# A diffusion backbone in fp32 on one core: taps laid out by the host, gate sums as columns, factors and modulation rows turned by transposes

## The chip, the cores and the metric

One core of a Trainium2 chip. The metric is the device time of one execution in microseconds, the median over the runs. The engines are named as in the profile: PE is TensorE's matrix multiply, PEld its weight load, DVE VectorE, ACT ScalarE, POOL GpSimd, SP SyncE, which issues nearly all the transfers of this kernel.

## What is computed

Two layers over 1024 latent rows of 1024 channels, with a context of 256 rows. The first is attention in a window of 128 with a sink and rotary positions, the second a conformer module with a depthwise convolution of 31 taps. Both begin with an RMS norm that is modulated by a shift and a scale, and end with a gate, all three made from the conditioning vector c.

```python
def reference(x, c, ctx, c_ctx, ada_w, ada_b, norm_g, attn_w_in, attn_sink, attn_w_out,
              conv_w_in, conv_b_in, conv_dw_w, conv_dw_b, conv_ln_g, conv_ln_b, conv_w_out, final_g):
    silu_c, silu_cc = jax.nn.silu(c), jax.nn.silu(c_ctx)
    for i in range(DEPTH):                      # 0: attention, 1: convolution
        shift, scale, gate = jnp.split((silu_c @ ada_w[i] + ada_b[i])[:, None, :], 3, axis=-1)
        h_lat = modulate(rmsnorm(x, norm_g[i]), shift, scale)        # h * (1 + scale) + shift
        if kind == 0:                           # h_ctx: the same of the context, with silu_cc
            y, y_ctx = attention_layer(h_lat, h_ctx, attn_w_in[j], attn_sink[j], attn_w_out[j], cos, sin, ctx_out)
        else:
            y = conformer_conv_branch(h_lat, *conv_args)
        x = x + gate * y
    return rmsnorm(x, final_g)

def conformer_conv_branch(h, w_in, b_in, dw_w, dw_b, ln_g, ln_b, w_out):
    a, gl, z = jnp.split(h @ w_in + b_in, 3, axis=-1)
    u = a * jax.nn.sigmoid(gl)
    u = depthwise_conv(u, dw_w) + dw_b          # 31 taps a channel, 2048 channels
    u = jax.nn.silu(layernorm(u, ln_g, ln_b))
    return (u * jax.nn.silu(z)) @ w_out
```

## The kernel before, in words

Every large product is made in three: each operand is split in a high and a low part of a rounded fp32 type, and high by high, low by high and high by low add up in PSUM (hh_page, hl_page with whi_page, wlo_page in attention's projections; h2h_page, h2l_page in the convolution's; gs_page, ozh_page, ozl_page with woh_page, wol_page in the output projections). These 512-column products make up most of what TensorE does. The small products that the change is about are plain fp32, and each of them stands in the trace as two records; a transpose stands as one.

- **Prologue.** The rows of x are normed and turned, k step by k step (kt 0 to 7). In the meantime `ada_mm` (line 408) makes shift and scale of the first layer as rows: for a k step of 256 channels four partial sums stand in partitions 0, 32, 64 and 96, c and the context's c in two neighbouring rows each. VectorE copies that to arow_half (`ada_row`, 420). `ada_cols` (424) makes columns of it: two plain products with `sel`, a 128x2 table of ones, add up the four partial sums and turn them at once; two operations on VectorE add the bias and write `mod`. Behind these stands the chain of x's tile: hf_page and hh_page (x times scale plus shift), hl_page (their difference), and TensorE's products. The upper half of x is scaled by a row of factors `rb1` instead: line 619 spreads the four columns of r1 over 128 partitions by four plain products with the identity.
- **Attention.** 16 heads by 8 blocks, with the projections' products filled in between (`fill`). The rest of the conditioning, `ada_rest` (672), runs beside it on VectorE: for 16 groups of 256 columns (four gate groups of layer 0, then the twelve groups of layer 1, of which the last four are its gate) eight multiply-adds over loads of ada_w, a copy to acc_a, and then a sum over the 128 partitions on TensorE. For shift and scale of layer 1 this is two products of 128x1, whose columns are copied to `mod1` (707 to 709). For a gate it is one product of ones with the row of 256, a copy of that row and a transfer to `gd` in HBM (702 to 705). `gate_rows` (1374) reads `gd` later, spread over the partitions (gate_page), for the output projections.
- **Taps.** At the end of attention the two tables dwr_page are cleared on POOL, the taps are loaded into their first 31 rows, and `turn_taps` (1390) turns them in four steps, each of four transposes and a copy to `dww`, between the products of attention's output projection (`later`). `sum_taps` (1424) then makes `wsum`, the sums of neighbouring taps. dww and wsum lie in the memory that `ada_rest` used for its loads (660).
- **Convolution and norm.** TensorE makes the projections of 16 channel blocks, VectorE, POOL and ACT the taps (`conv_dve`, `conv_pool`), and then `layer_norm` (1553) for two halves of the rows; it spreads its factor r by four plain products with the identity (1588), multiplies sixteen pages by it, and the output projection follows.

The order of the engines is the program's own: line 91 is the helper that pins an instruction of an engine in program order, so nearly all instructions carry this line in the profile, and they are told apart by their tiles. A scheduler places what isn't pinned, loads on SP among them.

Of the kernel before, what the change touches and what calls it, by code (L numbers as in the profile page):

```python
# [9 lines left out]
F32 = mybir.dt.float32  # L10
F32R = mybir.dt.float32r
AF = mybir.ActivationFunctionType
ALU = mybir.AluOpType

P = 128
# [10 lines left out]
NJ = CW // P  # L26
TAPS = 31
# [69 lines left out]
def backbone_kernel(  # L97
    ctx_stack: ExitStack,
    tc: tile.TileContext,
    x, ctx, ada_w, attn_sink, attn_w_out, conv_dw_w, conv_w_out, final_g,  # L100
    k_rows, k_vecs, k_ada, k_win, k_wconv, k_xt,
    k_cos, k_sin, k_mask, k_ident,
    out,
):
# [28 lines left out]
    def ps_o(i=None):  # L133
        if i is None:
            oflip[0] ^= 1
            i = oflip[0]
        return ps.tile([P, 512], F32, tag=f"o{i}", name=nm("pso"), bufs=1)
# [10 lines left out]
    def ctile(shape, dt, name):  # L148
        return cpool.tile(shape, dt, tag=name, name=name, bufs=1)
# [7 lines left out]
    def tt(eng, out, a, b, op):  # L157
        return eng.tensor_tensor(out=out, in0=a, in1=b, op=op)
# [10 lines left out]
    sink = ctile([P, 16], F32, "sink")[:, 0:NH]  # L169
    nsink = ctile([P, NH], F32, "nsink")  # L170
    ones = ctile([P, P], F32, "ones")
    dww = ctile([P, NJ, TAPS], F32, "dww")
    pt = ptpool.tile([P, 5280], F32R, tag="pt", name="pt", bufs=1)
    pthi, ptlo = (pt[:, i * 2560:i * 2560 + 2560].rearrange("p (a b) -> p a b", b=P) for i in range(2))
    acc_a = c2pool.tile([P, 352], F32, tag="acc_a", name="acc_a", bufs=1)[:, 0:256]
# [159 lines left out]
    for kt in range(3, 6):  # L335
        ada_load(kt)

    cs = ctile([P, 40], F32, "cs")[:, 0:16]
    tp = ps_g()
    PE.transpose(tp[:, 0:48], crow, ident[0:48, 0:48])  # L340
    act(cs, tp[:, 0:16], AF.Silu)
# [82 lines left out]
    def ada_cols(kt):  # L424

        rw, m = R[kt // 2], mods[kt]
        cps = ps_o(1)
        for j in range(2):
            c0 = kt % 2 * 256 + j * P
            PE.matmul(cps[:, 2 * j:2 * j + 2], rw[:, c0:c0 + P], sel, start=True, stop=True)  # L430
        if kt % 2:
            hp.free(R.pop(kt // 2))
        with tc.high_priority():
            V.tensor_scalar(out=m[:, 0], in0=cps[:, 0:2], scalar1=bcol[:, kt:kt + 1], scalar2=None, op0=ALU.add)
            V.tensor_scalar(out=m[:, 1], in0=cps[:, 2:4], scalar1=bcol[:, 8 + kt:9 + kt], scalar2=vt[:, 96 + kt:97 + kt],
                            op0=ALU.add, op1=ALU.mult)

    def turn(ts, kt, bank):
# [140 lines left out]
    for kt in range(2, KT):  # L579
        nx = kt + 1  # L580
        if 2 < kt < KT - 1:
            ada_row(nx)
            tp = turn(xs0, nx, ps_g) if nx < KT - 1 else turn_apart(xs0[0:2], nx, ps_g())
        if kt == 5:
            root1 = rstd_root(ss1, D, 4)
        if kt == KT - 1:
            x_mm(kt - 1, 0, acc0, (2,))
            turn_vecs()
            for n in (2, 0, 1):
                x_mm(kt, 0, acc0, (n,), (0,))  # L590
        x_mm(kt, 0, acc0, (0,), {2: (0,), KT - 1: (1, 2)}.get(kt, range(3)))
        if nx == KT - 1:
            tp = tp, turn_apart(xs0[2:4], nx, ps_o(0))
        if nx < KT:
            ada_cols(nx)
            if kt == 5:
                r1 = rstd_end(root1, 4)
            if nx < KT - 1:
                x_tile(tp, nx, 0, V)
            else:  # L600
                x_tile_apart(tp, nx)
        else:
            x_h(0)
            x_f(1)
            x_l(0)
            rc = rstd_end(rootc, 2)
        if kt == 2:
            x_mm(kt, 0, acc0, (0,), (1, 2))
        if nx < KT:
            x_mm(kt, 0, acc0, (1,))  # L610
            x_mm(kt - 1, 0, acc0, (2,), range(3) if kt > 2 else (2,))
        else:
            x_mm(kt, 0, acc0, (2, 1), (1, 2))
        for i in {3: (0, 1), 4: (2, 3)}.get(kt, ()):
            square(xs1[i], ss1[:, i:i + 1], A)
        if kt == 4:
            pg.free(*xs1)
        if kt == 5:
            rps = ps_o(1)
            for b in range(4):  # L620
                PE.matmul(rps[:, b * P:b * P + P], r1[:, b:b + 1].to_broadcast([P, P]), ident, start=True, stop=True)
            rb_pg = pg.alloc(F32, [1024], "rb")
            rb1 = rb_pg[:, 0:512]
            act(rb1, rps, AF.Copy)
            for i in range(2):
                square(cx[i], ssc[:, i:i + 1], A)
        if kt == 6:
            pg.free(*xs0)
            cos, sin = (pg.alloc(F32, [1024], n) for n in ("cos", "sin"))
            SY.dma_start(out=cos, in_=k_cos)  # L630
            SY.dma_start(out=sin, in_=k_sin)
            rootc = rstd_root(ssc, D, 2)
            x_f(0)
# [38 lines left out]
    def ada_rest():  # L672
        todo = [(l, c0) for l, c0 in [(0, 2048 + 256 * i) for i in range(4)] + [(1, 256 * i) for i in range(12)]]
        todo = [(l, c0, kt) for l, c0 in todo for kt in range(KT)]

        def load(i):
            l, c0, kt = todo[i]
            SY.dma_start(out=ada_raw[i % 2], in_=ada_w[l, kt * P:(kt + 1) * P, c0:c0 + 256])

        load(0)  # L680
        bank = ps_o(1)
        acc, o = bank[:, 0:256], bank[:, 256:512]
        for i, (l, c0, kt) in enumerate(todo):
            if i + 1 < len(todo):
                load(i + 1)
            raw = ada_raw[i % 2]
            if kt == 0:
                after(V.tensor_scalar(out=acc, in0=raw, scalar1=cs[:, kt:kt + 1], scalar2=None, op0=ALU.mult))
                for b in range(2):
                    col = (c0 - 2048 if l == 0 else 1024 + c0) // P + b  # L690
                    bs = slice(b * P, b * P + P)
                    stt(acc[:, bs], ident, abt[:, col:col + 1], acc[:, bs], ALU.mult, ALU.add)
            else:
                after(stt(acc, raw, cs[:, kt:kt + 1], acc, ALU.mult, ALU.add))
            yield
            if kt < KT - 1:
                continue
            V.tensor_copy(acc_a, acc)
            yield "copied"
            if i + 1 == len(todo):  # L700
                yield
            if c0 >= 2048:
                PE.matmul(o[0:1], ones[:, 0:1], acc_a, start=True, stop=True)
                V.tensor_copy(acc_a[0:1], o[0:1])
                SY.dma_start(out=gd[l][:, c0 - 2048:c0 - 1792], in_=acc_a[0:1])
            else:
                for b in range(2):
                    PE.matmul(o[:, b:b + 1], acc_a[:, b * P:b * P + P], ones[:, 0:1], start=True, stop=True)
                V.tensor_copy(mod1[:, c0 // P:c0 // P + 2], o[:, 0:2])

    adag = ada_rest()
# [670 lines left out]
    gbc0.append(gate_rows(0))  # L1382


    dwr = pg.alloc(F32, [1024], "dwr"), pg.alloc(F32, [1024], "dwr")
    for i in range(2):
        G.memset(dwr[i][0:32, :], 0.0)
        SY.dma_start(out=dwr[i][0:TAPS, :], in_=conv_dw_w[0, :, i * 1024:(i + 1) * 1024])

    def turn_taps(q):  # L1390
        o = ps_o()
        for i in range(4):
            j = q * 4 + i
            PE.transpose(o[:, i * 32:(i + 1) * 32], dwr[j // 8][0:32, (j % 8) * P:(j % 8 + 1) * P], ident[0:32, 0:32])
        V.tensor_copy(dww[:, q * 4:q * 4 + 4, :], o[:, 0:128].rearrange("p (a b) -> p a b", b=32)[:, :, 0:TAPS])
        if q == 3:
            pg.free(*dwr)
            sum_taps()

    for q in range(4):  # L1400
        later.append(lambda q=q: turn_taps(q))


    border = []
    nz = 0
# [15 lines left out]
        G.memset(u[:, :, 520:528], 0.0)  # L1421
    wsum = ctile([P, NJ, 16], F32, "wsum")

    def sum_taps():
        V.tensor_copy(wsum[:, :, 0:1], dww[:, :, 0:1])
        tt(V, wsum[:, :, 1:16], dww[:, :, 2:31:2], dww[:, :, 1:30:2], ALU.add)

    dwb2 = ctile([P, NJ], F32, "dwb2")
    V.tensor_scalar(out=dwb2, in0=vt[:, 48:64], scalar1=2.0, scalar2=None, op0=ALU.mult)
# [123 lines left out]
    def layer_norm(half):  # L1553
# [31 lines left out]
        yield "spread"  # L1585
        rb = ps_o(bank)
        for b in range(4):
            PE.matmul(rb[:, b * P:b * P + P], r[:, b:b + 1].to_broadcast([P, P]), ident, start=True, stop=True)
        yield 4.0
        for j in range(NJ):  # L1590
            v = vh(j, half)
# [379 lines left out]
def _columns(w):  # L1971
    return w.reshape(KT, P, -1, P).transpose(2, 1, 0, 3)


def _laid_out(i):
    rows = [i["c"], i["c_ctx"], i["norm_g"], i["ada_b"][0, 0:2 * D]]
    vecs = [i["conv_b_in"], i["conv_dw_b"], i["conv_ln_g"], i["conv_ln_b"], i["ada_b"][0, 2 * D:], i["ada_b"][1]]
    ada = i["ada_w"][0, :, 0:2 * D].reshape(2, 4, P, 2, KT, P).transpose(4, 0, 2, 1, 3, 5).reshape(KT, 2, P, 4, 2 * P)
    return {"k_rows": np.concatenate([v.reshape(-1, P) for v in rows]),
            "k_vecs": np.concatenate([v.reshape(-1, P) for v in vecs]),  # L1980
            "k_ada": ada, "k_win": _columns(i["attn_w_in"][0]), "k_wconv": _columns(i["conv_w_in"][0]),
            "k_xt": i["x"][0, 512:].reshape(512, 4, 2, P).transpose(1, 3, 2, 0)}


_INS = ["x", "ctx", "ada_w", "attn_sink", "attn_w_out", "conv_dw_w", "conv_w_out", "final_g"]
_OUTS = [((1, T, D), "float32")]


# [18 lines left out]
```

## Time and profile before

| | |
|---|---|
| median of 3 runs | 1678.72 us (1678.7 to 1679.17) |
| the profiled execution | 1680.83 us, its span 1679.1 us |
| granted TensorE clock over the span | 0.999 of full speed |
| PE busy | 1666.0 us (99%), 8340 instructions |
| PEld | 1396.3 us (83%) |
| DVE | 1091.2 us (65%), 2063 instructions |
| ACT | 870.2 us (52%) |
| POOL | 874.9 us (52%) |
| DVE in 40 slices, tenths | 5755554555455554556234389999999999868832 |
| DMA | 244.63 MB, mean 146 GB/s; 139607 packets |

A record of TensorE begins before the one ahead of it has ended, so lengths of records don't add up to time; the distance from one start to the next does. The span leaves out some 1.7 us that the execution's time holds. Shares of busy time are averages over stages; where an engine waits, and for what, is read from the timeline.

### The profile page before, as it was taken

The numbers are of one execution on the slowest core, as the hardware profiler recorded it, in microseconds if no ns is written. First come the engines' busy times: TensorE is split into PE (matmuls) and PEld (weight loads), VectorE is DVE, ScalarE is ACT, GpSimd is POOL, SyncE is SP. The second block draws the span as 40 slices with busy tenths as digits, with TensorE's granted clock in tenths as the row PEclk, the third lists the DMA queues.
The fourth block names the chain that finished last, engine by engine and source line by source line (L and its number), as shares of the span: only waits on it lengthen the run. The fifth ranks groups of instructions, "written<-read, shape, count | busy, mean of one in ns | idle before, by whom it ended". The sixth has DMA issues, their size and how long they took to land.

```text
span 1679.1 us, 23843 instructions
## 1 busy us (share of the span) xinstructions
PE 1666.0 (99%) x8340; PEld 1396.3 (83%) x8340; DVE 1091.2 (65%) x2063; ACT 870.2 (52%) x1523; POOL 874.9 (52%) x831
## 2 busy tenths in 40 slices
PE   9999999999999999999999999999999999999998
PEld 6888888888888888888888788888888888888886
DVE  5755554555455554556234389999999999868832
ACT  5644543555355544546333365555665664566731
POOL 0246673576547564642001268999898887130400
PEclk9999999999999999999999999999999999999999
DMA  9424442444335443457976522020211212387981
GB/s 382 171 62 144 141 144 76 142 154 151 105 125 167 148 129 98 127 159 262 325 247 215 193 88 101 1 76 14 76 50 51 88 38 70 132 276 246 318 288 50
DMA packets 139607, 244.63 MB, mean 146 GB/s; under 512 B 44650, under 2 KB 61346, under 8 KB 139488
## 3 DMA queue, kind: packets, MB, share of 16 engines
q1 hardware_dynamic: 133408, 233.15, 40.7%
q10 hardware_dynamic: 6080, 9.97, 2.4%
q8 instruction: 65, 1.06, 0.2%
q14 instruction: 54, 0.44, 0.1%
HBM read 190.90 MB, written 41.69 MB: 139 GB/s over the span
## 4 chain that ended last, share of the span: by engine, by line
PE 97%; DVE 1%; DMA 1%; POOL 0%; ACT 0%; issue 0%; ACTq 0%; POOLq 0%; DVEq 0%
PE psg L91 50%; PE pss L91 26%; PE pso L91 22%; DMA rope_half<-rope_half 1%; POOL rope_half L91 0%; DVE rq L91 0%; DVE x_page L91 0%; DVE ms L91 0%; DVE rope_half L91 0%; POOL kl_page L91 0%; DVE wlo_page L91 0%; ACT whi_page L91 0%; ACTq L91 0%; ACT rope_half L91 0%; DVE hf_page L91 0%
## 5 line engine op out<-in xcount | busy, mean ns | idle before, releaser
L91 POOL TENSOR_TENSOR odd_half<-odd_half,prod_half 128x513 f32<-128x513 f32 (+2 forms) x252 | 314.5, 1256 | 22.5 <-ACT prod_half L91 9.2
L91 POOL TENSOR_TENSOR wlo_page<-wraw_page,whi_page 128x512 fp32r<-128x512 f32 (+1 forms) x104 | 174.9, 1698 | 157.2 <-ACT whi_page L91 125.7
L91 PE MATMUL psg<-hh_page,whi_page 128*128 128x512 f32 x600 | 236.8, 395 | 0.0
L91 PE MATMUL psg<-hl_page,whi_page 128*128 128x512 f32 x600 | 234.8, 391 | 0.0
L91 PE MATMUL psg<-hh_page,wlo_page 128*128 128x512 f32 x600 | 234.3, 390 | 0.0
L91 ACT ACTIVATE prod_half<-ubuf,dww 128x513 f32<-128x513 f32 (+2 forms) x252 | 165.6, 675 | 116.7 <-POOL odd_half L91 113.0
L91 PE MATMUL psg<-h2h_page,whi_page 128*128 128x512 f32 x464 | 181.9, 392 | 0.0
L91 PE MATMUL psg<-h2h_page,wlo_page 128*128 128x512 f32 x464 | 180.6, 389 | 0.0
L91 PE MATMUL psg<-h2l_page,whi_page 128*128 128x512 f32 x464 | 180.6, 389 | 0.0
L91 DVE SCALAR_TENSOR_TENSOR pss<-ubuf,dww,pss 128x512 f32<-128x512 f32 (+3 forms) x270 | 173.0, 674 | 0.1
L91 DVE SCALAR_TENSOR_TENSOR pss<-ubuf,wsum,pss 128x512 f32<-128x512 f32 (+3 forms) x270 | 172.3, 674 | 0.2
L91 ACT ACTIVATE pt<-pss 128x640 fp32r<-128x640 f32 (+1 forms) x128 | 86.7, 677 | 142.5 <-PE pss L91 142.5
L91 POOL TENSOR_SCALAR p_page<-p_page,sc 128x576 f32<-128x576 f32 (+2 forms) x128 | 93.2, 728 | 106.9 <-DVE sc L91 104.4
L91 ACT ACTIVATE p_page<-p_page,sc 128x577 f32<-128x577 f32 (+2 forms) x128 | 96.9, 757 | 78.6 <-DVE sc L91 76.7
L91 DVE CUSTOM_DVE_ANT_0 p_page<-pss,mask_page,nsink 128x576 f32<-128x576 f32 (+1 forms) x112 | 90.2, 806 | 70.5 <-PE pss L91 57.4
L91 PEld LDWEIGHTS psg<-hh_page,wlo_page 128*128 128x128 f32 x600 | 112.7, 188 | 24.2
L91 PEld LDWEIGHTS psg<-hh_page,whi_page 128*128 128x128 f32 x600 | 112.7, 188 | 19.7 <-ACT hh_page L91 0.3
L91 PEld LDWEIGHTS psg<-hl_page,whi_page 128*128 128x128 f32 x600 | 113.0, 188 | 19.1 <-DVE hl_page L91 0.2
L91 DVE TENSOR_TENSOR pt<-pss,pt 128x640 fp32r<-128x640 f32 (+1 forms) x128 | 100.7, 787 | 36.3 <-ACT pt L91 36.1
L91 ACT ACTIVATE whi_page<-wraw_page 128x1024 fp32r<-128x1024 f32 x88 | 92.6, 1052 | 53.9 <-PE psg L91 19.3
L91 PE MATMUL pso<-h2h_page,whi_page 128*128 128x512 f32 x304 | 118.3, 389 | 0.0
L91 PE MATMUL pso<-h2l_page,whi_page 128*128 128x512 f32 x304 | 118.3, 389 | 0.0
(255 smaller groups left out, 3915.6 us busy)
## 6 DMA issues: line engine op xcount, KB each, us to landing
wraw_page<-in_k_wconv_dram SPq DMA_DIRECT2D x48, 512.0 KB
wraw_page<-in_k_win_dram SPq DMA_DIRECT2D x40, 512.0 KB
wo_page<-in_attn_w_out_dram SPq DMA_DIRECT2D x32, 512.0 KB
wol_page<-wolA SPq DMA_DIRECT2D x32, 512.0 KB
wo_page<-in_conv_w_out_dram SPq DMA_DIRECT2D x32, 512.0 KB
wol_page<-wolC SPq DMA_DIRECT2D x32, 512.0 KB
rope_half<-rope_half ACTq DMA_DIRECT2D x76, 128.0 KB
araw_page<-in_k_ada_dram SPq DMA_DIRECT2D x16, 512.0 KB
```

Of the source, the lines that this page charges most:

```text
L91: r = f(*a, **k)
```

## The change

Four edits. The host lays the taps out as [128, 16, 31] (`k_taps`), and one transfer loads `dww` as it is needed: tables, memsets, transposes and copies go, and `wsum` is made directly behind it. All sixteen groups of `ada_rest` are summed as two columns; a gate's columns are copied to `gcol` (128x2) and written to `gd` from there, element by element. The two spreads of `layer_norm` and the one of r1 are transposes of the spread column in place of products of it with the identity. `ada_cols` turns arow_half by two transposes, and a new reduction on VectorE adds the four partial sums, ahead of the two operations that write `mod` (they now read SBUF).

```diff
@@ -97,8 +97,8 @@
...
-    x, ctx, ada_w, attn_sink, attn_w_out, conv_dw_w, conv_w_out, final_g,
-    k_rows, k_vecs, k_ada, k_win, k_wconv, k_xt,
+    x, ctx, ada_w, attn_sink, attn_w_out, conv_w_out, final_g,
+    k_rows, k_vecs, k_ada, k_win, k_wconv, k_taps, k_xt,
@@ -169,7 +169,6 @@
...
     ones = ctile([P, P], F32, "ones")
-    dww = ctile([P, NJ, TAPS], F32, "dww")
     pt = ptpool.tile([P, 5280], F32R, tag="pt", name="pt", bufs=1)
@@ -335,7 +334,7 @@
...
 
-    cs = ctile([P, 40], F32, "cs")[:, 0:16]
+    cs = ctile([P, 16], F32, "cs")[:, 0:16]
     tp = ps_g()
@@ -427,12 +426,15 @@
...
             c0 = kt % 2 * 256 + j * P
-            PE.matmul(cps[:, 2 * j:2 * j + 2], rw[:, c0:c0 + P], sel, start=True, stop=True)
+            PE.transpose(cps[:, j * P:j * P + P], rw[:, c0:c0 + P], ident)
         if kt % 2:
...
         with tc.high_priority():
-            V.tensor_scalar(out=m[:, 0], in0=cps[:, 0:2], scalar1=bcol[:, kt:kt + 1], scalar2=None, op0=ALU.add)
-            V.tensor_scalar(out=m[:, 1], in0=cps[:, 2:4], scalar1=bcol[:, 8 + kt:9 + kt], scalar2=vt[:, 96 + kt:97 + kt],
+            su = small([P, 2, 2], name="adasum")
+            V.tensor_reduce(out=su, in_=cps[:, 0:2 * P].rearrange("p (j g r) -> p j r g", j=2, g=4)[:, :, 0:2],
+                            axis=mybir.AxisListType.X, op=ALU.add)
+            V.tensor_scalar(out=m[:, 0], in0=su[:, 0], scalar1=bcol[:, kt:kt + 1], scalar2=None, op0=ALU.add)
+            V.tensor_scalar(out=m[:, 1], in0=su[:, 1], scalar1=bcol[:, 8 + kt:9 + kt], scalar2=vt[:, 96 + kt:97 + kt],
                             op0=ALU.add, op1=ALU.mult)
@@ -618,7 +620,7 @@
...
             for b in range(4):
-                PE.matmul(rps[:, b * P:b * P + P], r1[:, b:b + 1].to_broadcast([P, P]), ident, start=True, stop=True)
+                PE.transpose(rps[:, b * P:b * P + P], r1[:, b:b + 1].to_broadcast([P, P]), ident)
             rb_pg = pg.alloc(F32, [1024], "rb")
@@ -699,13 +701,13 @@
...
                 yield
+            for b in range(2):
+                PE.matmul(o[:, b:b + 1], acc_a[:, b * P:b * P + P], ones[:, 0:1], start=True, stop=True)
             if c0 >= 2048:
-                PE.matmul(o[0:1], ones[:, 0:1], acc_a, start=True, stop=True)
-                V.tensor_copy(acc_a[0:1], o[0:1])
-                SY.dma_start(out=gd[l][:, c0 - 2048:c0 - 1792], in_=acc_a[0:1])
+                gcol = small([P, 2], name="gcol", bufs=1)
+                V.tensor_copy(gcol, o[:, 0:2])
+                SY.dma_start(out=gd[l][:, c0 - 2048:c0 - 1792].rearrange("o (b p) -> p (o b)", p=P), in_=gcol)
             else:
-                for b in range(2):
-                    PE.matmul(o[:, b:b + 1], acc_a[:, b * P:b * P + P], ones[:, 0:1], start=True, stop=True)
                 V.tensor_copy(mod1[:, c0 // P:c0 // P + 2], o[:, 0:2])
@@ -1382,24 +1384,8 @@
...
 
-    dwr = pg.alloc(F32, [1024], "dwr"), pg.alloc(F32, [1024], "dwr")
-    for i in range(2):
-        G.memset(dwr[i][0:32, :], 0.0)
-        SY.dma_start(out=dwr[i][0:TAPS, :], in_=conv_dw_w[0, :, i * 1024:(i + 1) * 1024])
-
-    def turn_taps(q):
-        o = ps_o()
-        for i in range(4):
-            j = q * 4 + i
-            PE.transpose(o[:, i * 32:(i + 1) * 32], dwr[j // 8][0:32, (j % 8) * P:(j % 8 + 1) * P], ident[0:32, 0:32])
-        V.tensor_copy(dww[:, q * 4:q * 4 + 4, :], o[:, 0:128].rearrange("p (a b) -> p a b", b=32)[:, :, 0:TAPS])
-        if q == 3:
-            pg.free(*dwr)
-            sum_taps()
-
-    for q in range(4):
-        later.append(lambda q=q: turn_taps(q))
-
+    dww = ctile([P, NJ, TAPS], F32, "dww")
+    SY.dma_start(out=dww, in_=k_taps)
 
@@ -1421,9 +1407,8 @@
...
 
-    def sum_taps():
-        V.tensor_copy(wsum[:, :, 0:1], dww[:, :, 0:1])
-        tt(V, wsum[:, :, 1:16], dww[:, :, 2:31:2], dww[:, :, 1:30:2], ALU.add)
+    V.tensor_copy(wsum[:, :, 0:1], dww[:, :, 0:1])
+    tt(V, wsum[:, :, 1:16], dww[:, :, 2:31:2], dww[:, :, 1:30:2], ALU.add)
 
@@ -1585,7 +1570,7 @@
...
         for b in range(4):
-            PE.matmul(rb[:, b * P:b * P + P], r[:, b:b + 1].to_broadcast([P, P]), ident, start=True, stop=True)
+            PE.transpose(rb[:, b * P:b * P + P], r[:, b:b + 1].to_broadcast([P, P]), ident)
         yield 4.0
@@ -1979,10 +1964,11 @@
...
+            "k_taps": i["conv_dw_w"][0].T.reshape(NJ, P, TAPS).transpose(1, 0, 2),
-_INS = ["x", "ctx", "ada_w", "attn_sink", "attn_w_out", "conv_dw_w", "conv_w_out", "final_g"]
+_INS = ["x", "ctx", "ada_w", "attn_sink", "attn_w_out", "conv_w_out", "final_g"]
```

On VectorE, at the first k step of the prologue (arow_half are the modulation rows, hf_page and hl_page the tile of x), before:

```order
12 L91 COPY arow_half_104<-pso_241 128x256
13 L91 TENSOR_SCALAR mod_181<-pso_259,bcol 128x2
14 L91 TENSOR_SCALAR mod_181<-pso_259,bcol,vt 128x2
15 L91 TENSOR_TENSOR wlo_page_271<-wraw_page_109,whi_page_270 128x1024
16 L91 TENSOR_SCALAR hf_page_276<-psg_255,mod_181 128x512
17 L91 TENSOR_TENSOR hl_page_275<-hf_page_276,hh_page_274 128x512
```

and now:

```order
12 L91 COPY arow_half_103<-pso_240 128x256
13 L91 TENSOR_REDUCE adasum_261<-pso_258 128x4
14 L91 TENSOR_SCALAR mod_180<-adasum_261,bcol 128x2
15 L91 TENSOR_SCALAR mod_180<-adasum_261,bcol,vt 128x2
16 L91 TENSOR_TENSOR wlo_page_272<-wraw_page_108,whi_page_271 128x1024
17 L91 TENSOR_SCALAR hf_page_277<-psg_254,mod_180 128x512
18 L91 TENSOR_TENSOR hl_page_276<-hf_page_277,hh_page_275 128x512
```

One instruction is new, between the turned rows in PSUM and `mod`; the order of the rest stays, here and at the seven other k steps.

On TensorE, in attention's output projection (woh_page and wol_page are the weight's parts), before:

```order
3477 L91 MATMUL pss_8124<-wol_page_7663,ozh_page_7733 128x512
3478 L91 MATMUL pss_8124<-woh_page_7731,ozl_page_7734 128x512
3479 L91 MATMUL pso_8150<-ident,dwr_page_8102 128x32 x4
3480 L91 MATMUL pso_8156<-ident,dwr_page_8102 128x32 x4
3481 L91 MATMUL pss_8124<-woh_page_7803,ozh_page_7805 128x512
3482 L91 MATMUL pss_8124<-wol_page_7726,ozh_page_7805 128x512
```

and now:

```order
3477 L91 MATMUL pss_8153<-wol_page_7692,ozh_page_7762 128x512
3478 L91 MATMUL pss_8153<-woh_page_7760,ozl_page_7763 128x512
3479 L91 MATMUL pss_8153<-woh_page_7832,ozh_page_7834 128x512
3480 L91 MATMUL pss_8153<-wol_page_7755,ozh_page_7834 128x512
3481 L91 MATMUL pss_8153<-woh_page_7832,ozl_page_7835 128x512
```

The transposes of the taps are gone from between the products, and so is the second run of eight further on.

On SP, at the end of attention (gd is the gate in HBM, ozd and xr_page belong to the output projection), before:

```order
329 L91 DMA wo_page_7943<-in_attn_w_out_dram 128x2x512
330 L91 DMA gate_page_8100<-gd_609 128x1024
331 L91 DMA gd_610<-acc_a 1x256
332 L91 DMA xr_page_8201<-in_x_dram 128x512 x2
333 L91 DMA dwr_page_8102<-in_conv_dw_w_dram 31x1024
334 L91 DMA ozd<-oz_half_7976 128x4x64 x2
335 L91 DMA dwr_page_8103<-in_conv_dw_w_dram 31x1024
336 L91 DMA wol_page_8237<-wolA 128x1024
```

and now:

```order
329 L91 DMA wo_page_7974<-in_attn_w_out_dram 128x2x512
330 L91 DMA dww<-in_k_taps_dram 128x496
331 L91 DMA gate_page_8131<-gd_624 128x1024
332 L91 DMA gd_625<-gcol_7948 128x2x1
333 L91 DMA wol_page_8222<-wolA 128x1024
334 L91 DMA ozd<-oz_half_8007 128x4x64 x2
335 L91 DMA xr_page_8203<-in_x_dram 128x512 x2
```

The load of dww stands ahead of the read of gate_page, the gate is written from columns, and wol_page and xr_page have changed places.

## Rows read from the trace of the kernel before

**Rows 1.** The page, chain that ended last: shares of the span by engine.

```profile
PE 97%; DVE 1%; DMA 1%; POOL 0%; ACT 0%; issue 0%; ACTq 0%; POOLq 0%; DVEq 0%
```

**Rows 2.** The chain in order of time, convolution: start us, us, what.

```profile
1023.81 5.44 PE pso L91 x24
```

**Rows 3.** Timeline of PE, a gate and a mod1 site: start, us, operation, tiles, forms.

```profile
122.66 0.71 PE L91 MATMUL pss<-ident,p_page 128*128 128x128 f32 x5
123.29 0.59 PE L91 MATMUL pso<-acc_a,ones 128*1 128x256 f32 x2
...
124.07 0.28 PE L91 MATMUL pss<-kvc_page,qh_page 128*128 128x256 f32 x1
...
305.71 0.71 PE L91 MATMUL pss<-ident,p_page 128*128 128x128 f32 x5
306.25 0.50 PE L91 MATMUL pso<-ones,acc_a 128*128 128x1 f32 x4
...
306.85 0.28 PE L91 MATMUL pss<-kvc_page,qh_page 128*128 128x256 f32 x1
```

**Rows 4.** Timeline of PE, the first run of tap transposes.

```profile
809.08 0.39 PE L91 MATMUL pss<-woh_page,ozl_page 128*128 128x512 f32 x1
809.40 0.68 PE L91 MATMUL pso<-ident,dwr_page 32*128 32x32 f32 x8
...
810.35 0.40 PE L91 MATMUL pss<-wol_page,ozh_page 128*128 128x512 f32 x1
```

**Rows 5.** Timeline of DVE, end of attention (in brackets: the wait ahead, and what ended it).

```profile
789.19 0.69 DVE L91 SCALAR_TENSOR_TENSOR oz_half<-pso,zs_page 128x512 f32<-128x512 f32 x1 [3.60 <-PE pso L91]
```

**Rows 6.** Timeline of PE, a spread of layer_norm and four transposes.

```profile
1466.10 1.05 PE L91 MATMUL pso<-ident,r 128*128 128x128 f32 x8
1466.91 0.48 PE L91 MATMUL psg<-h2h_page,whi_page 128*128 128x512 f32 x1
...
977.70 0.60 PE L91 MATMUL pso<-ident,xn_page 128*128 128x128 f32 x4
978.05 0.48 PE L91 MATMUL psg<-h2h_page,whi_page 128*128 128x512 f32 x1
```

**Rows 7.** Timelines of PE, DVE, ACT: a plain turn, its reader; two transposes, theirs.

```profile
31.31 0.50 PE L91 MATMUL pso<-ident,arow_half 128*128 128x2 f32 x4
...
30.52 0.42 DVE L91 COPY arow_half<-pso 128x256 f32<-128x256 f32 x1
31.85 0.22 DVE L91 TENSOR_SCALAR mod<-pso,bcol 128x2 f32<-128x2 f32 x1 [0.91 <-PE pso L91]
...
261.67 0.38 PE L91 MATMUL pso<-ident,vf_half 128*128 128x128 f32 x2
...
262.08 0.39 ACT L91 ACTIVATE kvc_page<-pso 128x256 fp32r<-128x256 f32 x1
```

**Rows 8.** Timelines of DVE and PE in the prologue: hl_page, r, and who takes them.

```profile
18.16 0.50 PE L91 MATMUL pss<-hl_page,whi_page 128*128 128x512 f32 x1 [0.16 <-DVE hl_page L91]
...
29.91 0.69 DVE L91 TENSOR_TENSOR hl_page<-hf_page,hh_page 128x512 fp32r<-128x512 f32 x1
...
30.84 0.39 PE L91 MATMUL pss<-hl_page,whi_page 128*128 128x512 f32 x1
...
41.01 0.16 DVE L91 SCALAR_TENSOR_TENSOR r<-rq,rr 128x4 f32<-128x4 f32 x1
...
41.39 1.05 PE L91 MATMUL pso<-ident,r 128*128 128x128 f32 x8
```

**Rows 9.** Timelines of DVE (convolution), POOL and PE (a score block); the page's DMA queues.

```profile
1159.92 0.75 DVE L91 SCALAR_TENSOR_TENSOR ubuf<-pso,vt,sig_page 128x512 f32<-128x512 f32 x1 [0.73 <-PE pso L91]
...
175.16 0.71 POOL L91 TENSOR_SCALAR p_page<-p_page,sc 128x512 f32<-128x512 f32 x1
...
178.39 0.60 PE L91 MATMUL pss<-ident,p_page 128*128 128x128 f32 x4
...
q1 hardware_dynamic: 133408, 233.15, 40.7%
```

## The prediction

> **What bounds the kernel now.** I read the page first. TensorE is busy for 99% of the span, and the chain of waits leads through it for 97% with nothing put down to issue [rows 1]: an instruction taken from TensorE's own queue is worth its time, if what comes next on TensorE is ready. I therefore priced every edit from start to start: from the first instruction touched to the next one that is not, since the records overlap and their lengths don't add. The unit is the distance of two 512-column products, 5.44 us for 24 of them, 0.227 us [rows 2]. Then I looked, site by site in the timelines of TensorE and of VectorE, at how long the next operand had been waiting.
>
> **Gate sums.** At the eight gate sites one product of ones with a row of 256 stands in two records between the transposes of p_page and the score products. From the first transpose to the product on kvc_page, 122.66 to 124.07, go 1.41 us. The sites of mod1 stand in the same surroundings and hold already the four 128x1 records that the change puts everywhere: 305.71 to 306.85 is 1.14 us [rows 3]. That is 0.27 us a site, and **2.16 us** for eight. VectorE's copy of one row of 256 becomes a copy of two columns. The DMA behind it writes the same 1 KB as 256 elements of four bytes; no row shows that, and it is a rival below. At nothing I take it because its readers, the two gate pages, come late.
>
> **Taps.** Sixteen transposes of 32 rows go from TensorE's queue, in two runs of eight: 809.08 to 810.35 is 1.27 us where two 512-column products alone take 0.454 [rows 2, 4]: 0.82 us a run, **1.63 us** in all. Four copies on VectorE and two memsets on POOL go too. wsum is now made earlier on VectorE and waits there for the tap load; what is queued behind it are score blocks and an ozl_page. But a few instructions on VectorE waits 3.60 us for TensorE anyway [rows 5], so a load that is late by up to that costs nothing, and each us beyond it one. On SP the one tap load passes the read of the gate page and the last gate write, and the loads of xr_page and wol_page change places; all are prefetches of tiles used several products later. One difference on VectorE falls behind sixteen multiplies in the third part of the norm; TensorE takes that page only after several other pages' products. I cost these moves at nothing; without their cover TensorE would wait for as long as the moved step takes.
>
> **Spreads.** Three times four plain 128x128 products (eight records) become four transposes. 1466.10 to 1466.91 is 0.81 us; four transposes of the same size, ahead of the same kind of product, take 977.70 to 978.05, 0.35 [rows 6]. That is 0.46 us each, **1.38 us**.
>
> **Modulation rows.** Eight times four records become two transposes. By the spreads (eight records to four) this is worth 0.23 us on TensorE each time. But behind the product hangs a chain: product, mod on VectorE, hf_page, hh_page, hl_page, and TensorE takes hl_page. The change lengthens it by a sum (TENSOR_REDUCE, 16 values to 4 a partition), which two operations of mod wait for. No row of this kernel shows such a sum. It can't cost less than the smallest row of its kind, r with 0.16 us on four columns out of SBUF [rows 8], and hardly more than the copy of 256 columns out of PSUM, 0.42 [rows 7]. I take 0.22, the row of mod on two columns out of PSUM [rows 7], since it reads the same bank and as little. Against it stands that transposes are done sooner: mod starts 0.54 us after its first product (31.31, 31.85), a reader of two transposes 0.41 after the first (261.67, 262.08) [rows 7]: 0.13 us. The chain grows by δ = 0.22 − 0.13 = 0.09 us; the ends give 0.03 and 0.29.
> What of the 0.23 stays depends on how long hl_page has lain ready. In kt 0, 1, 2 and 7 TensorE is already waiting for it (18.16 [rows 8] is the clearest): nothing stays. In kt 3 hl_page ends at 29.91 + 0.69 = 30.60 and is taken at 30.84, 0.24 us later; TensorE starts at best 0.05 after its releaser, so 0.19 stays, and kt 4 and 5 read alike. At kt 6 the spread is taken at 41.39, 0.22 after r (41.01 + 0.16) [rows 8], and 0.16 stays. The gain is 3 x 0.19 + 0.16 − 8δ = 0.73 − 0.72 = **0.01 us**; with the ends of δ +0.49 to −1.59.
>
> **The sum** is 2.16 + 1.63 + 1.38 + 0.01 = 5.18 us. The profiled execution took 1680.83 us, so it would take 1675.65; it lies 2.1 over the median of the runs, 1678.72, and the median becomes **1673.5**. With the ends of δ the sum is 5.66 to 3.58, and the forecast holds from 1673.1 to 1675.1.
>
> **Rivals.**
> 1. *The chain doesn't bind in the modulation.* If VectorE has the sum done inside the time that the transposes save, all eight sites keep 0.23 us: 1.84 in place of 0.01, 7.01 in all, **1671.7**. For it speaks that the hh_page products can be taken in the meantime; against it the waits on hl_page at four of the eight.
> 2. *A transpose costs its whole record.* Two transposes have 0.38 us, four 0.60 [rows 6, 7], so one alone has 0.38 − (0.60 − 0.38)/2 = 0.27 us. If each stood alone, a spread would take 1.08 us against 0.81, and lose 0.27 three times (−0.81); the modulation would lose the sum's 0.22 eight times (−1.76) with nothing back. 2.16 + 1.63 − 0.81 − 1.76 = 1.2, **1677.5**. The four at 977.70 have a successor after 0.35, which is against it.
>  The Trainium skill, "TensorE: Matmul & The Clock Gate", Part 4: PE-mode transpose, gives about 275 ns for a 128x128 transpose inside a kernel; by that price paid four times a spread takes 1.1 us, and this edit would be a loss. The trace agrees on the single record and not on the pitch.
> 3. *VectorE bounds the convolution.* By the slices of the page it is busiest there; if it sets the pace, all that is won before 977.70 [rows 6], where the second norm turns its rows and the convolution follows, is given back, and only the two later spreads stay, 0.92: **1677.8**. Against it: in that stretch VectorE waits 0.73 us for TensorE at 1159.92 [rows 9], and the products follow each other at 5.44 for 24 [rows 2].
> 4. *The gate writes block the queue (slower).* Eight writes go out as 256 packets of four bytes each on SP's DMA queue, with the loads of ada_w and of the next weights behind them. By the queue's row a packet takes 0.407 x 16 x 1679.1 / 133408 = 0.082 us on one of 16 engines [rows 9], and 16 packets an engine are 1.3 us a write, hidden: at such a site p_page ends at 175.16 + 0.71 = 175.87 and TensorE takes it at 178.39 [rows 9], 2.5 us later. It decides from 2.5 us a write on. At 0.3 us a packet a write takes 4.8 us, 2.3 past the cover, eight times 18.4: 1678.7 − 5.2 + 18.4 = **1692**. Against it: that is nearly four times what a packet takes here, and packets on average far larger.
>  The Trainium skill, "DMA: Bandwidth & Descriptors", Rules for kernel authors, warns of a last dimension that isn't contiguous (one descriptor per element), and its Specifications say that transfers under 512 B are read, modified and written. This speaks against the change; no run before shows such a write, and the page gives no time for one.
>
> That the change doesn't do what it says I give no chance: the listings ahead show the records gone.
>
> **How the numbers follow.** Forecast 0.65; rival 1 0.14; rival 2 0.05; rival 3 0.10; rival 4 0.06. 0.2% of this kernel, 3.4 us, is about what a measurement of it can tell from no change: faster is under 1675.4, slower over 1682.1. Forecast and rival 1 are faster (0.79), rivals 2 and 3 the same (0.15), rival 4 slower (0.06). The range takes in forecast and rival 1, 0.79 of the chance: from 1671.7 to 1675.1, widened by the 0.5 us (1678.7 to 1679.2) by which the runs of before differ, rounded: 1671.2 to 1675.6.
>
> **What would show it.** In the profile after, a gate site should read 1.14 us from the first p_page transpose to kvc_page; the two runs of products around the taps should follow at 0.227; each spread should read 0.35 for four records; mod should begin some 0.09 us later after its first transpose than now after its first product. At the end of the prologue the timeline should be ahead by the first spread's 0.46, at the second norm's transposes by 0.5 + 2.2 + 1.6, at the end by two spreads more. It is wrong if TensorE shows new waits for hl_page longer than 0.3 us in the first 50 us (the sum is dearer than taken), if p_page or a weight page is waited for behind a gate write (rival 4), or if TensorE's groups of 24 in the convolution stretch beyond 5.44 us (rival 3).

## The result, and the profile after

The changed kernel takes 1686.01 us in the median of five runs (1685.07 to 1687.42), the kernel before 1679.17 in five: a ratio of 1.0043, with a 95% interval of 1.003 to 1.0055. It is slower by 7 us where 5 us of gain were forecast.

The page's chain of waits of the kernel after, by engine, and what TensorE waited for (us in total, times, longest us):

```profile
PE 90%; DMA 5%; DVE 1%; ACT 1%; POOL 1%; issue 1%; SPq 0%; ACTq 0%; POOLq 0%; DVEq 0%
...
PE pss L91 <- POOL p_page L91: 4.1, 2, 2.1
PE psg L91 <- DVE rope_half L91: 3.5, 1, 3.5
...
PE pss L91 <- DVE sc L91: 0.7, 2, 0.5
```

Before, the chain was TensorE for 97% and transfers for 1% [rows 1], and of these waits TensorE had one:

```profile
PE pss L91 <- POOL p_page L91: 1.6, 1, 1.6
```

Now transfers hold 5% of the chain, p_page is waited for twice, and the waits for rope_half and sc (small columns of the softmax) are new. The instructions taken away are gone, though, and the sites read as forecast. TensorE's timeline at the first gate site, at the former place of the taps and at the first spread of layer_norm:

```profile
124.42 0.71 PE L91 MATMUL pss<-ident,p_page 128*128 128x128 f32 x5
124.96 0.51 PE L91 MATMUL pso<-ones,acc_a 128*128 128x1 f32 x4
...
125.56 0.28 PE L91 MATMUL pss<-kvc_page,qh_page 128*128 128x256 f32 x1
...
818.45 0.39 PE L91 MATMUL pss<-woh_page,ozl_page 128*128 128x512 f32 x1
818.67 0.39 PE L91 MATMUL pss<-woh_page,ozh_page 128*128 128x512 f32 x1
...
1473.17 0.60 PE L91 MATMUL pso<-ident,r 128*128 128x128 f32 x4
1473.53 0.48 PE L91 MATMUL psg<-h2h_page,whi_page 128*128 128x512 f32 x1
```

The gate site takes 1.14 us (1.41 in [rows 3]), the products around the taps follow at 0.22 [rows 4], the spread takes 0.36 for 0.81 [rows 6].

To find where the time went, TensorE's instructions of both traces can be laid side by side and the difference of their starts followed. It falls by 0.25 us at each of eight gate sites, by 0.81 at each place of the taps and by 0.45 at the first spread, and by 1.18 at 961.25, where the kernel before waits 1.0 us for x_page and this one does not. It jumps up at the instructions that stand in the kernel before at 174.76 (0.76 us), 178.75 (0.44), 222.36 (2.29) and 254.09 (3.66): 7.15 us of new waits, all in attention, behind the second, third and fourth gate write of layer 0. And three times it creeps up over a few us in which no engine is waited for: behind the instructions at 96.31, 222.36 and 254.09 by some 1.6 each. The table by stretches shows what that is, first of the kernel after, then of the kernel before (columns: us, busy us and instructions of five engines, granted clock, DMA share, GB/s):

```profile
90.00:97.00 7.00, 5.00 (x31) 4.14 (x29) 2.70 (x8) 4.04 (x8) 3.71 (x4) 1.00 0.16 37
97.00:101.00 4.00, 4.00 (x16) 3.38 (x15) 2.67 (x6) 1.56 (x4) 1.47 (x3) 0.57 0.11 33
...
227.00:231.00 4.00, 4.00 (x17) 3.66 (x17) 2.91 (x7) 2.18 (x5) 3.10 (x4) 0.57 0.40 93
...
265.00:268.00 3.00, 3.00 (x16) 3.00 (x16) 1.23 (x2) 0.63 (x1) 1.28 (x1) 0.50 0.38 90
```

```profile
97.00:101.00 4.00, 4.00 (x25) 3.49 (x25) 2.50 (x6) 1.79 (x5) 1.43 (x4) 1.00 0.12 33
```

Behind three waits, of 2.0, 2.1 and 3.5 us, the granted clock read 0.57, 0.57 and 0.50: TensorE worked at its lower level, 1.2 GHz, and then at full speed again, with 16 instructions in the first of these stretches where there were 25. The wait at 96.31 was there before with 1.6 us, and the clock held. It is 2.0 us in this execution; but in the trace of e1 (below) it is 2.0 us too, and the clock behind it stays at 1.00.

What is late behind a gate write? The chain in order of time of the kernel after, around the longest of the new waits, and the transfers of rope_half in that stretch, from issue to landing:

```profile
249.96 9.84 DMA rope_half<-rope_half
...
259.93 1.27 POOL rope_half L91
...
261.22 2.34 DVE rope_half L91 x2
...
263.61 4.63 PE psg L91 x24
...
DMA to landing us min/median/max: 2.2/9.3/9.8
```

A gate was written at 245.4. Transfers of rope_half, 128 KB each, issued 4 us later by another engine's queue (ACT's), took over 9 us where they take 2.4 in the median of the whole run, and TensorE waited at the end of their chain. The view of the transfers from 244 to 262 us (40 slices of 0.45 us; then KB each, median us to landing):

```profile
GB/s 373 382 228 382 400 365 38 0 75 84 5 0 18 18 7 50 39 30 30 36 5 16 25 46 18 18 337 405 387 257 198 221 162 153 21 0 0 132 159 0
...
wraw_page<-in_k_win_dram SPq DMA_DIRECT2D x1, 512.0 KB, 9.3
...
gd<-gcol SPq DMA_DIRECT2D x1, 1.0 KB, 8.8
```

From 249.4 to 255.7 us only 5 to 50 GB/s moved, though a load of wraw_page and the two transfers of rope_half had been issued, at 248.78 to 249.96; then it was 337 and more. The gate's 1 KB, issued at 245.41, landed after 8.8 us, at 254.2.

### The profile page after: what moved, and what is told of

Its sections match the earlier page's. It is cut to its first block, busy times and chain, and to the rows that moved or that the text cites. A ratio compares the mean times of both kernels' runs of the same rounds, so it can differ in the third digit from the quotient of the medians.

```text
span 1685.5 us, 23775 instructions
## 1 busy us (share of the span) xinstructions
PE 1666.0 (99%) x8312; PEld 1398.2 (83%) x8312; DVE 1087.3 (65%) x2067; ACT 868.4 (52%) x1523; POOL 872.1 (52%) x829
## 4 chain that ended last, share of the span: by engine, by line
PE 90%; DMA 5%; DVE 1%; ACT 1%; POOL 1%; issue 1%; SPq 0%; ACTq 0%; POOLq 0%; DVEq 0%
PE psg L91 48%; PE pss L91 23%; PE pso L91 20%; DMA rope_half<-rope_half 2%; DMA wraw_page<-in_k_win_dram 1%; DMA x_page<-in_x_dram 1%; DMA x_page<-in_ctx_dram 1%; DMA dww_raw<-in_ada_w_dram 1%; POOL rope_half L91 0%; DMA araw_page<-in_k_ada_dram 0%; DMA cos_page<-in_k_cos_dram 0%; DMA low_page<-in_attn_w_out_dram 0%; DVE rope_half L91 0%; ACT hf_page L91 0%; ACT hh_page L91 0%
```

## The experiments

Three theories stood at first. **Theory 1:** the writes of 256 four-byte elements hold up the transfers behind them. **Theory 2:** the loss comes from the order of VectorE, POOL and SP that the change moved. **Theory 3:** it comes from the quicker prologue, which lengthens the wait at 96 us and brings the clock down.

**e1_gate_only.** The kernel before with this edit alone:

```diff
+            for b in range(2):
+                PE.matmul(o[:, b:b + 1], acc_a[:, b * P:b * P + P], ones[:, 0:1], start=True, stop=True)
             if c0 >= 2048:
-                PE.matmul(o[0:1], ones[:, 0:1], acc_a, start=True, stop=True)
-                V.tensor_copy(acc_a[0:1], o[0:1])
-                SY.dma_start(out=gd[l][:, c0 - 2048:c0 - 1792], in_=acc_a[0:1])
+                gcol = small([P, 2], name="gcol", bufs=1)
+                V.tensor_copy(gcol, o[:, 0:2])
+                SY.dma_start(out=gd[l][:, c0 - 2048:c0 - 1792].rearrange("o (b p) -> p (o b)", p=P), in_=gcol)
```

> Before with the gate edit alone (columns, and the gate written as 256 elements of four bytes). Theory 1: the eight writes hold up every transfer for some us, and the transfers of rope_half and dww_raw behind them make TensorE wait and then run at half its clock: about 8 us slower than before, near 1687, with waits of TensorE for p_page and rope_half between 170 and 260 us. Theory 2 (the loss comes from the order of VectorE, POOL and SP that the whole change moved, not from the writes): 2 us faster than before by the eight sums, 1677. Theory 3 (the loss comes from the quicker prologue alone): also 1677.

Measured: 1689.63 us against 1679.46, ratio 1.0062 (1.0047 to 1.0077). Slower by 10 us, as theory 1 has it. What TensorE waited for:

```profile
PE pss L91 <- POOL p_page L91: 4.5, 2, 2.5
PE psg L91 <- DVE rope_half L91: 3.6, 1, 3.6
...
PE pss L91 <- DVE sc L91: 1.8, 1, 1.8
```

TensorE waits in the same places as in the whole change; the wait for sc is longer (1.8 us), and here the clock fell behind that one. The eight sums gave their 0.25 us each all the same. This shows that the gate edit is the cause; that it is the write in it, e9 and e10 show.

**e2_no_gate.** The change with the edit of e1 taken back.

> The change without its gate edit (row product, row copy, row write as before). Theory 1: no waits for rope_half or p_page between 170 and 260 us, and the time is that of before less taps (1.6), the wait for x_page at 961 (1.2) and the spreads (1.0), plus up to 1.9 if TensorE still drops to half its clock at 97 us: 1675.5 to 1677.5. Theory 2: still slow, 1684 or more. Theory 3: the drop at 97 us is there, 1677.5.

Measured: 1678.15 us against 1679.46, ratio 0.9995 (0.9985 to 1.0004), not to be told from no change. It lies 0.7 us above theory 1's range, and far from theory 2's 1684. No wait for rope_half; p_page is waited for once, 1.6 us as before. The 1.2 us for x_page that were counted there are no gain of the change: TensorE's wait for x_page stands in the one profiled execution of the kernel before, and in none of the traces made since, that of e1 among them.

**e3_gate_rows.** The change, with the gate written otherwise:

```diff
-                gcol = small([P, 2], name="gcol", bufs=1)
-                V.tensor_copy(gcol, o[:, 0:2])
-                SY.dma_start(out=gd[l][:, c0 - 2048:c0 - 1792].rearrange("o (b p) -> p (o b)", p=P), in_=gcol)
+                g0 = (c0 - 2048) // P
+                V.tensor_copy(gcol[:, g0:g0 + 2], o[:, 0:2])
+                if g0 == 6:
+                    PE.transpose(o[0:8, 0:P], gcol, ident)
+                    V.tensor_copy(acc_a[0:8, 0:P], o[0:8, 0:P])
+                    SY.dma_start(out=gd[l].rearrange("o (b p) -> (o b) p", p=P), in_=acc_a[0:8, 0:P])
```

> The change whole, but a layer's eight gate columns are gathered in SBUF, turned by one transpose and written once as eight rows of 512 bytes. The order of the engines is that of the change but for these few instructions. Theory 1: the waits between 170 and 260 us go (7.2 us and two drops of the clock, 3.3): 1675 to 1676. Theory 2: stays at 1685 to 1686, since the order is the same.

Measured: 1676.93 us, ratio 0.9986 (0.9976 to 0.9995), 9 us under the change. It is 0.9 us over the range expected. The order on every engine is that of the change but for these instructions and the places of three small operations of VectorE next to them, so theory 2 falls. From 240 to 262 us the transfers of rope_half land in time again:

```profile
DMA to landing us min/median/max: 2.2/2.4/3.9
```

**e4_prologue_only.** Before, with `ada_cols` and the spread of r1 as in the change, nothing else.

> Before with the modulation rows and the first spread turned by transposes, nothing else. Theory 3: the prologue gains 0.2 to 0.5 us, the wait for p_page at 96 us grows from 1.6 to 2.0 us, and TensorE falls to half its clock behind it, which costs 1.5 us: 1680.5 to 1681. If the clock holds: 1679, no more than the wait takes back. Theories 1 and 2: no waits beyond 100 us that before does not have.

Measured: 1681.5 us, ratio 1.0007 (0.9997 to 1.0017), unclear. Its ten runs fall in two groups, four from 1679.51 to 1680.16 and six from 1681.38 to 1681.99, about 2 us apart, which is near the price of one drop of the clock. The profiled execution is one of the faster: TensorE waits 2.2 us for p_page, and the clock holds (1.00 from 97 to 101 us). So theory 3 doesn't account for the 7 us. What sets the slower group apart stays open: that its clock drops isn't shown, and the granted clocks of the runs read 0.998 or 0.999 in both groups (0.996 in the change's profiled execution, with its three drops).

**e5_write_forms.** What in the write is dear? One kernel, four forms of a 1 KB write, each at two sites.

```diff
+        if kind == "A":
+            SY.dma_start(out=flat[0:256].rearrange("(b p) -> p b", p=P).unsqueeze(2), in_=c.unsqueeze(2))
+        elif kind == "B":
+            SY.dma_start(out=d.rearrange("(b p) c -> p b c", p=P)[:, :, 0:1], in_=c.unsqueeze(2))
+        elif kind == "C":
+            SY.dma_start(out=flat[0:256].rearrange("(p b) -> p b", p=P), in_=c)
+        else:
+            SY.dma_start(out=d[0:2, :].rearrange("a b -> (a b)").unsqueeze(0), in_=acc_a[0:1, 0:256])
```

> The kernel of e3_gate_rows with one more 1 KB write to unused memory at each of the eight gate sites, in four forms, each twice: A 256 elements of four bytes side by side (as the change writes), C 128 runs of eight bytes, B 256 elements of four bytes 512 bytes apart, D one row of 1 KB; in the order A, C, B, D, D, B, C, A. (The content of the writes is not used by anything.) If the standstill is a price per element, A and B take alike, some 6 to 11 us from issue to landing, C half of what they take above D, and D 2 to 3 us. If it comes from many small writes to the same lines of memory, A and C are slow and B lands like D. The 1 KB form D costs nothing under either.

Measured: 1676.87 us in its one run. The view of the transfers, in the stretches of C (163 us), B (198), B (706), C (740):

```profile
dum<-probe SPq DMA_DIRECT2D x1, 1.0 KB, 5.3
...
dum<-probe SPq DMA_DIRECT2D x1, 1.0 KB, 1.5
...
dum<-probe SPq DMA_DIRECT2D x1, 1.0 KB, 1.6
...
dum<-probe SPq DMA_DIRECT2D x1, 1.0 KB, 5.0
```

B, with as many elements as the change writes, lands in 1.5 and 1.6 us. C takes 5.3 and 5.0, but at two other sites, where more is under way: at these two B takes 5.7 and 3.6 us in e10 (below). So C shows no clear price for its 128 runs. The landings of A and D aren't in this trace; A is compared with B in e9 and e10. The kernel wasn't slowed: its A's stand at the first and the last site, where the change shows no new wait either.

**e9_writes_side_by_side** and **e10_writes_apart.** e3 with A at all eight sites, and e3 with B at all eight. Every engine issues the same instructions in both, in the same order but for two neighbouring operations of ScalarE that have changed places; in the program only the addresses differ.

> e3_gate_rows with one more write at each of the eight gate sites, 256 elements of four bytes side by side in unused memory: the write of the change, beside a kernel that doesn't need it. If the write itself is the cause, the waits for rope_half and p_page between 170 and 260 us come back, and the time is 8 to 10 us over e3: 1685 to 1687. If it mattered only that the gate's own data came late, nothing changes: 1677.

> The same 256 elements of four bytes, the same queue and the same order of every engine, but in memory 512 bytes apart. By e5 such a write lands in 1.5 us, so if the cause is the neighbours in one line of memory and not the number of elements, the time is that of e3: 1676.5 to 1677.5. If the number of elements decides, it is that of e9.

Measured: e9 1685.91 us, ratio 1.0033 (1.002 to 1.0046); e10 1677.27 us, ratio 0.9982 (0.9972 to 0.9992). The same write costs 8.6 us more when its elements lie side by side; 512 bytes apart, the time can't be told from e3's 1676.93. In e9, the transfers of the write over the whole run, two of TensorE's waits, and the transfers at the third of the eight gate sites (198 to 206 us), where little else is under way:

```profile
dum<-probe SPq DMA_DIRECT2D x8, 1.0 KB, 9.6
...
PE pss L91 <- POOL p_page L91: 4.4, 2, 2.3
PE psg L91 <- DVE rope_half L91: 2.8, 1, 2.8
...
wraw_page<-in_k_win_dram SPq DMA_DIRECT2D x1, 512.0 KB, 8.9
...
dww_raw<-in_ada_w_dram SPq DMA_DIRECT2D x1, 128.0 KB, 9.1
dum<-probe SPq DMA_DIRECT2D x1, 1.0 KB, 9.4
```

and in e10, with the transfers at the third site (197 to 205 us) and then the write at the two sites where e5 has C (162 to 170 us, 739 to 747):

```profile
dum<-probe SPq DMA_DIRECT2D x8, 1.0 KB, 2.8
...
PE pss L91 <- POOL p_page L91: 1.4, 1, 1.4
...
wraw_page<-in_k_win_dram SPq DMA_DIRECT2D x1, 512.0 KB, 3.2
...
dww_raw<-in_ada_w_dram SPq DMA_DIRECT2D x1, 128.0 KB, 2.0
...
dum<-probe SPq DMA_DIRECT2D x1, 1.0 KB, 1.7
...
dum<-probe SPq DMA_DIRECT2D x1, 1.0 KB, 5.7
...
dum<-probe SPq DMA_DIRECT2D x1, 1.0 KB, 3.6
```

In e9 nothing reads what the write leaves, so it isn't the gate's data that come late; it is the others' transfers: at the third site a load of 512 KB lands after 8.9 us behind A and after 3.2 behind B.

**e6_rows_no_prologue, e7_late_turn_no_prologue, e8_late_turn.** Is there a version that beats both? In e3 TensorE waited 0.5 us in all for the last copy to gcol, so e7 and e8 issue the turn one step later; e6 and e7 leave the prologue as before.

```diff
                 if g0 == 6:
+                    yield
                     PE.transpose(o[0:8, 0:P], gcol, ident)
```

> e3_gate_rows with the modulation rows and the first spread put back to plain products. If the prologue's edit is lost at the p_page wait at 96 us, and costs a drop of the clock there in some executions, this is as fast as e3 or up to 1 us faster in the median, and its executions lie closer together: 1676 to 1677. If the prologue's gain is kept, it is 0.5 us slower than e3: 1677.4.

> e6 with the transpose of the gate columns issued one step later, so that TensorE does not wait for the copy of the last columns (0.3 us at two sites in e3): 0.5 to 0.8 us faster than e6, 1675.5 to 1676.

> e3 with the transpose of the gate columns issued one step later, prologue as in the change: 0.5 to 0.8 us faster than e3, 1676.2; against e7 it shows once more what the prologue's edit is worth.

Measured: e6 1677.7 us, ratio 0.9986 (0.9977 to 0.9995); e7 1675.28, 0.9976 (0.9967 to 0.9985); e8 1676.06, 0.9978 (0.9969 to 0.9986); the kernel before 1679.95. e7 and e8 beat both kernels, by 4.7 and 3.9 us against before. The late turn gave e7 2.4 us over e6, more than expected; I don't know what the rest is, as it shifts every later step of `ada_rest` by one. With and without the prologue's edit can't be told apart (e7 and e8). Nor did e6 lie closer together than the others: 1676.31 to 1678.87.

## Why the prediction was wrong

**The step that failed** is in the gate sums: of the write of 256 elements the prediction says "At nothing I take it because its readers, the two gate pages, come late." The readers of that write were never late. It holds up the transfers of others. By the jumps of TensorE's starts it cost 7.15 us of waits and two drops of the clock with 1.6 each, 10.3 us; by e9 against e10 8.6; by the change against e3 9.1.

**Rival 4 had the place and the sign, and its price was wrong.** It took 0.082 us a packet, spread over 16 engines, 1.3 us a write, and had a chance of 0.06. That is the mean over packets of all sizes to many addresses. Side by side the write is dearer: at the third site it lands in 9.4 us where the same elements apart take 1.7, 7.7 us more, which would be 0.030 us for each of the 256 if they are paid one after another. That they are isn't shown: only the spacings of 4 and 512 bytes were compared, and C is no clear third point. So a write takes some 9 us in place of 1.3, over three times its cover of 2.5 us. The rival also named only a part of those that wait: not only the loads behind it on SP's queue, but rope_half on ACT's.
The Trainium skill, "DMA: Bandwidth & Descriptors", Rules for kernel authors and Specifications, advises against a last dimension that isn't contiguous and gives 512 B as the least transfer for full rate; this spoke against the change. The runs bear out the advice for the change's own write, but not as a rule on size or count: e10's write has the same 256 elements of four bytes, and no cost of it shows in the time (1677.27 us against e3's 1676.93).

**Not every write hurt.** Those of layer 1 take as long (7.7 to 11 us from issue to landing), and TensorE waits for nothing there; the new waits stand behind three of the eight, those of layer 0 behind which rope_half, dww_raw or low_page were wanted at once. The rival's "eight times" was too much, and its 1692 as well. Nor did the rest of the change give all that was forecast: without the dear write e3 is 2.5 us faster than before and e10 3.3, of 5.2.

**The terms on TensorE were right, but for the second spread of layer_norm.** Gate sums 8 x 0.25 = 2.0 us (2.16 forecast). Taps 2 x 0.81 = 1.6 (1.63). The first spread of layer_norm 0.45 (0.46). The second kept 0.13 of 0.46 in this execution: it starts when r is ready, and TensorE came earlier than r. In e10 it kept 0.44; in e3 TensorE waited 1.2 us for r there and was 0.9 us later behind it. The prediction didn't ask whether r would be ready.

**δ was right, and the prologue gave less than forecast.** VectorE in the fourth step of the prologue, after:

```profile
30.76 0.42 DVE L91 COPY arow_half<-pso 128x256 f32<-128x256 f32 x1
31.88 0.17 DVE L91 TENSOR_REDUCE adasum<-pso 128x4 f32<-128x16 f32 x1 [0.71 <-PE pso L91]
32.09 0.23 DVE L91 TENSOR_SCALAR mod<-adasum,bcol 128x2 f32<-128x2 f32 x1
```

The first transpose started at 31.46, so the sum starts 0.42 us behind it, and mod at 0.63 where it was 0.54 [rows 7]: δ is 0.09, as forecast, though the sum is cheaper than taken (0.17 for 0.22) and the distance between the two operations makes it up. But of the 0.47 us forecast for the prologue TensorE had 0.2 at 60 us: at the last k step it now waits 0.2 us for hh_page, which is made from mod. Behind 96 us it had none in this execution, since the wait for p_page there was longer, 2.0 us for 1.6; behind it the clock fell, which cost 1.6 us more. That the prologue's edit lengthens this wait, as theory 3 has it, isn't shown. The wait stands at the end of a chain that begins with transfers of rope_half, and it differs from trace to trace: with the old prologue it is 1.5 to 2.0 us (2.0 in e1), with the new one 1.4 (e10) to 2.3 (e5). In e3 and e10 what TensorE is ahead of the kernel before stays about the same across it: 0.7 us ahead of the wait, 0.6 and 0.8 behind. The clock fell there in the change's trace alone.

**Rivals 1 to 3** did not come true: hl_page still sets the pace of the prologue (behind the sites of kt 3 to 5 TensorE is 0.07, 0.08 and 0.09 us ahead of the kernel before, so the 0.23 us of each are not kept), transposes follow each other at 0.09 us, and TensorE's difference to before stays within 0.05 us from 970 to 1460 us, through the convolution.

## What to carry to other kernels

Before a column is written to memory element by element, ask where its elements land: 256 neighbours of four bytes took 9.4 us to land where the same elements 512 bytes apart took 1.7, and other transfers waited meanwhile, on another queue too. Turn the column on TensorE first (one transpose and one copy for 1024 values here) and write rows. Ask not only who reads what a transfer leaves, but what else is under way beside it. And before a wait is put down to an edit, look at the same wait in other traces: the one at 96 us was 1.5 to 2.0 us long with the old prologue and 1.4 to 2.3 with the new.

## What the runs showed of the hardware that was not expected

- 256 writes of four bytes land in 9.6 us (median of e9's) when they lie side by side in 1 KB, and in 2.8 us (e10's) when they lie 512 bytes apart; at the quiet third site in 9.4 and 1.7. The records of the write's own packets don't show it: 9 ns each, in e9 as in e10.
- Behind a write on SP's queue two 128 KB transfers of ACT's queue landed after 9.3 and 9.8 us; in e10 the same two took at most 3.9.
- Behind waits of 1.8 us (e1) to 3.6 the granted clock fell to half, and each fall cost some 1.6 us. It didn't after every such wait: in e4 it held at full speed behind 2.2 us.
- A sum of 16 values to 4 a partition out of PSUM takes VectorE 0.17 us.
